# Splitting each mixer pass in two and starting the next pass beside the last delta-rule block, with looser pins on the row steps

## The chip, the cores and the metric

The kernel runs on one core of one Trainium2 chip. The metric is the device time of one execution in microseconds, the median of several runs.

## The reference

One residual block over 1024 tokens of width 1024, in float32, with one layer:

```python
h  = rmsnorm(x)
x += W_out [ gated delta rule, 4 heads x 128 | RG-LRU, 8 groups x 64 ](h)   # the mixer
x += cross_attention(rmsnorm(x), rmsnorm(mem))                              # 4 heads, 256 memory tokens
x += peer(rmsnorm(x))                                                       # 8 heads x 16 experts of 16384
out = rmsnorm(x)
```

In the mixer, q, k and v come from a projection, a causal convolution over 4 positions and SiLU. The delta rule keeps a 128x128 state for each head and goes over the tokens in order. The last part, `peer`, chooses for each token 8 x 16 experts by product keys; every expert is one row of a table `u` and one row of a table `v` (16384 x 1024 each), and adds `gate * gelu(u_e . x) * v_e`.

## The kernel before

**Mixer.** It goes over the tokens in four passes of T = 256 tokens (two blocks of 128). `mixer` (L414) does one pass: transposes of the normalised input (`transposed`, L431), the small projection for gates, twelve projections with convolution (L460; j = 0..3 is q, 4..7 is k, 8..11 is v, each 8 matmuls of 256 columns), a side stream (L472: the z projections and the RG-LRU half), then the delta rule for block b = 0 and block b = 1 (L590), which is a long chain of small matmuls, VectorE (DVE) products and ScalarE (ACT) copies. Then comes the output projection (`out`, L523, 8 weight tiles). While block b = 1 runs, the next input is loaded (L607); after the pass's y is complete it is normalised (L738), and the next pass begins when the output projection is emitted.

**Attention and expert choice.** A second stream, `attended` (L1243), goes over units of tokens (128, 128, 256, 256, 256) once the mixer has finished them: cross-attention, the expert queries, the two-level top-16 (`top16`), and then a choice stream (`choose`, L846).

**Gates.** Tokens 256 to 767 are done densely: over all 16384 experts with a gate matrix that is mostly zero. `gates` (L942) builds that matrix from one-hot products in 32 groups of 16 tokens, and writes each group to DRAM. It begins after the last mixer pass (the mixer's SBUF pool is closed, L1233) and, for each 256 tokens, after their choice is done.

**Dense stage.** `dense` (L1020) goes over 128 slices of 128 experts. Each slice loads a piece of `u` and of `v`, splits both in two halves (DVE `ul`, `vl`), makes 24 matmuls for the hidden values (`dh`), multiplies by gelu and gates (DVE `dg`, `dal`) and makes 24 matmuls for the output (`po`), part of which DVE adds up (`acc`).

**Row steps.** The other 512 tokens (four blocks of 128) are done by gathering rows: for every one of 128 expert slots, an indirect DMA from POOL (`fetch`, L1125) brings 128 rows of `u`, later of `v`, into one of six buffers `rb`, and one DVE instruction of 128x1024 uses it (`step`, L1142): 1024 such steps in all. They are filler: all streams are emitted by a planner that keeps an estimated clock for each engine, and each time the planned TensorE (PE) time has advanced by `pe.pace`, one step is emitted (L115 to L121): every 2800 planned ns in passes 0 to 2, 3500 in pass 3 and in the gates, 2250 in the dense stage. `keep_in_program_order` (L1153, L1164) pins a step behind all DVE work emitted before it; a scheduler that orders each engine's instructions by its own estimate may otherwise move an instruction ahead of work that isn't ready.

**What sets the order.** `together` (L1180) picks among the streams by rank, and among equals by the PE time they had over their share (6 for the mixer and its sides, 1 for attention and choices). A stream that has yielded a wait isn't ready until its engines are, by the planner's clocks.

Of the kernel before, what the change touches and what calls it, by code (L numbers as in the profile page):

```python
# [14 lines left out]
OP = mybir.AluOpType  # L15
AX = mybir.AxisListType

D = 1024
S = 1024
T = 256  # L20
NB = T // 128
NP = S // T
D0 = T
TD = 2 * T
# [13 lines left out]
SHARE = (6.0, 1.0, 6.0, 1.0)  # L38
L_NORM, L_STEP, L_CONV, L_SOFT, L_GATE = 14000.0, 2500.0, 4000.0, 6000.0, 1500.0
PACES = (2800.0, 2800.0, 2800.0, 3500.0)  # L40
PACE_G, PACE_D = 3500.0, 2250.0
FIRST = 0
EARLY = T
UNITS = ((0, 1), (128, 1), (256, 2), (512, 2), (768, 2))
# [5 lines left out]
def block_kernel(ctx: ExitStack, tc: tile.TileContext, a):  # L50
# [21 lines left out]
    class Engine:  # L72

        def __init__(self, engine, fixed, rate):
            self.engine, self.fixed, self.rate = engine, fixed, rate
            self.at = self.total = self.end = 0.0

        def __getattr__(self, op):
            call = getattr(self.engine, op)

            def f(*args, **kw):
                r = call(*args, **kw)  # L82
                aps = [x for x in list(args) + list(kw.values()) if isinstance(x, bass.AP)]
                if op == "dma_start":
                    moved(prod(args[0].shape) * 4)
                else:
                    self.spend(aps)
                return r
            return f

# [314 lines left out]
    def load_x(qkv, t0):  # L405
        for b, t in enumerate(blocks_of(qkv[:, 4:12, :])):
            sp.dma_start(t, a["x"][t0 + b * 128:t0 + (b + 1) * 128, :])

    def norm_x(fp, qkv):
        X = blocks_of(qkv[:, 4:12, :])  # L410
        junk = fp.tile([128, NB, 4, 128], F, name="zs", bufs=1)
        norm(X, NB, X, junk.rearrange("p a b c -> p (a b c)"))

    def mixer(fp, t0, qkv):  # L414
        def conv(ps, ti, w, out, bias=0.0):

            buf = fp.tile([128, T + 3], F, name="cbuf", bufs=CB)
# [7 lines left out]
        def tmp():  # L425
            return fp.tile([128, T], F, name="cy", bufs=CB)

        hT = fp.tile([128, 8, T], F, name="hT", bufs=1)
        if t0 < EARLY:
            hT = Pair(hT, low(0), tmp)  # L430
        yield from transposed(hT, blocks_of(qkv[:, 4:12, :]), NB, wmixc)  # L431
# [25 lines left out]
        dve.tensor_scalar(beta, beta, 1.0, 0.5, op0=OP.add, op1=OP.mult)  # L457


        for j in range(12):  # L460
            ps = yield from proj_T("wA", j, hT, T)
            y = fp.tile([128, T], F, name="cy", bufs=CB)
            conv(ps, j, hcw[:, j, :], y)
            th = fp.tile([128, T], F, name="cth", bufs=1)
            act.activation(th, y, AF.Tanh)
            dve.scalar_tensor_tensor(qkv[:, j, :], th, 1.0, y, op0=OP.add, op1=OP.mult)

        zs = fp.tile([128, NB, 4, 128], F, name="zs", bufs=1)
        yl = fp.tile([128, 4, T], F, name="yl", bufs=1)
        ready = set()  # L470

        def side():  # L472

# [44 lines left out]

        yield Stream(side(), RANK[2], SHARE[2])

        y, x1 = Both(qkv[:, 0:4, :], yl), []

        def out(b0, b1):  # L523

# [65 lines left out]
        for b in range(NB):  # L590
# [14 lines left out]
                act.activation(vb[:, h, :], tv[:, h, :], AF.Copy, scale=beta[:, b, h:h + 1])  # L605
            if b == NB - 1 and t0 + T < S:
                load_x(qkv, t0 + T)  # L607
            yield L_STEP
            pk = b4("tp")
            for h in range(H):  # L610
# [121 lines left out]
            if t0 == 0 and b == 0:  # L732
                yield Stream(out(0, 1), FIRST, SHARE[0])

        while not ready >= {"y", *range(NB)}:
            yield None
        if t0 + T < S:
            norm_x(fp, qkv)  # L738
        yield from out(0 if t0 else 1, NB)
        while t0 not in done:  # L740
            yield None

    def add_cols(X, j, ps):
# [359 lines left out]

    todo, fetched = [], []
    blocks = {}

    def add_block(row, rs, idx, gt):
# [29 lines left out]
    def late_row():  # L1139
        return bool(fetched) and fetched[0][4] > max(dve.at, pe.at) + WAIT  # L1140

    def step():  # L1142
        while todo and len(fetched) < NROW - 1:
            fetch()
        if not fetched:
            return False
        row, ph, k, t, _ = fetched.pop(0)
        B = blocks[row]
        if ph == "u":
            if k == 0:  # L1150
                dve.scalar_tensor_tensor(B["h"], B["h"], B["rs"], B["w"], op0=OP.mult, op1=OP.mult)
                B["hd"] = gat.tile([128, 128], F, name="hdot", bufs=1)
            tc.keep_in_program_order(  # L1153
                dve.scalar_tensor_tensor(t, t, 1.0, B["h"], op0=OP.mult, op1=OP.mult,
                                         accum_out=B["hd"][:, k:k + 1]))
            if k == 120:
                B["x"] = row_of(NROW + 1)
                sp.dma_start(B["x"], x2d[row:row + 128, :])
            if k == 127:
                B["a"] = gat.tile([128, 128], F, name="ga", bufs=1)  # L1160
                act.activation(B["a"], B["hd"], AF.Gelu_apprx_tanh)
                dve.tensor_mul(B["a"], B["a"], B["gt"].rearrange("p h k -> p (h k)"))
        else:
            tc.keep_in_program_order(  # L1164
                dve.scalar_tensor_tensor(B["x"], t, B["a"][:, k:k + 1], B["x"], op0=OP.mult, op1=OP.add))
            if k == 127:
                finish(B["x"], row, t)
        return True
# [58 lines left out]

    def mixed():

        for i in range(NP):  # L1230
            pe.pace = PACES[i]
            yield from mixer(fp, i * T, qkv)
        mix.close()  # L1233
        pe.pace = PACE_G
        yield Stream(gated(), RANK[3], SHARE[3])
# [28 lines left out]
    fps.close()  # L1264
    with tc.tile_pool(name="dn", bufs=1, side="right") as d2, \
            tc.tile_pool(name="dps", bufs=1, space=bass.MemoryType.PSUM) as dps:
        pe.pace, pe.real = PACE_D, False
        dense(dn[0], d2, dps, hT, raws)
    while step():
        pass  # L1270
# [64 lines left out]
```

## Time and profile before

| | us |
|---|---|
| median of 3 runs | 3276.9 |
| range of the runs | 3274.99 to 3279.72 |
| the profiled execution, its own time | 3275.43 |
| its span in the trace | 3273.7 |

| stretch of the span, us | what runs |
|---|---|
| 0 to 341 | pass 0, memory projections, first attention unit |
| 341 to 662 | pass 1, second unit; first row steps |
| 662 to 1009 | pass 2, third unit |
| 1009 to 1341 | pass 3, third and fourth unit |
| 1341 to 1790 | gates, rest of the fourth unit, fifth unit |
| 1790 to 3249 | dense stage |
| 3249 to 3274 | last sums, norms and stores |

PE is busy for 91% of the span, DVE for 84%, ACT for 39%, POOL for 44%. A busy share of a stretch says how full an engine is there, not who waits for whom; for that the views of waits and of the last chain are read beside it.

### The profile page before, as it was taken

What the parts mean: (1) busy time and instruction counts of PE and PEld (TensorE: products, weight loads), DVE (VectorE), ACT (ScalarE), POOL (GpSimd) and SP (SyncE); (2) the same over time, 40 slices, a digit from 0 to 9 for tenths busy, and PEclk for the clock granted to TensorE, in tenths of its full rate; (3) what the DMA queues carried; (4) which work ended last, traced back from release to release, by engine and by line L of the source; (5) the groups of instructions that cost most, each with busy time, mean ns of one, the idle gap of its engine ahead of it and who ended that gap; (6) DMA issues with size and microseconds to landing.
All of it is one profiled execution on the core that took longest, in us unless ns stands there. A gap on an engine that the chain in (4) does not pass through costs nothing.

```text
span 3273.7 us, 46519 instructions
## 1 busy us (share of the span) xinstructions
PE 2987.4 (91%) x16212; PEld 2559.6 (78%) x16212; DVE 2737.6 (84%) x5999; ACT 1277.8 (39%) x2694; POOL 1431.4 (44%) x1046
## 2 busy tenths in 40 slices
PE   6999997699999989898857899999999999999998
PEld 6888887678988878887746677888888878888886
DVE  7634776877787898898999798888999989899998
ACT  6843363236322642376357332222222222222222
POOL 0000233334433344243345375556666655566663
PEclk9999998899999999998968899999999999999999
DMA  5346788688888769888888799999999899999995
GB/s 170 110 143 208 248 281 308 232 285 284 308 292 291 251 223 332 301 281 302 303 289 273 267 329 334 333 340 330 344 333 328 319 334 333 330 341 327 339 331 198
DMA packets 321547, 941.66 MB, mean 288 GB/s; under 512 B 28912, under 2 KB 108832, under 8 KB 319264
## 3 DMA queue, kind: packets, MB, share of 16 engines
q0 software_dynamic: 148048, 538.04, 46.8%
q1 hardware_dynamic: 107216, 367.08, 30.9%
q10 hardware_dynamic: 66048, 33.56, 3.7%
q8 instruction: 128, 2.10, 0.3%
q14 instruction: 107, 0.88, 0.1%
HBM read 894.53 MB, written 44.04 MB: 287 GB/s over the span
## 4 chain that ended last, share of the span: by engine, by line
PE 61%; DVE 20%; DMA 9%; ACT 5%; issue 3%; POOL 1%; SPq 0%; ACTq 0%; DVEq 0%; POOLq 0%
PE dh L106 21%; PE po L106 20%; PE pj L106 15%; DVE rb L82 6%; DMA rb<-in_u,idx 4%; PE gd L106 3%; DVE oh L82 3%; DMA gd<-stage 2%; DMA w<-in_pwq 1%; PE tp L111 1%; PE sc L106 1%; DVE cy L82 1%; ACT ohg L82 1%; DVE i L82 1%; ACT L82 1%
## 5 line engine op out<-in xcount | busy, mean ns | idle before, releaser
L1134 POOL DMA_INDIRECT rb<-in_u,idx x512 | 677.4, 1323 | 1111.9 <-DVE rb L82 497.0
L1134 POOL DMA_INDIRECT rb<-in_v,idx x512 | 745.0, 1455 | 690.3 <-DVE rb L82 478.7
L82 DVE SCALAR_TENSOR_TENSOR rb<-rb 128x1024 f32<-128x1024 f32 x512 | 613.1, 1218 | 90.2 <-DMA rb<-in_u,idx 90.2
L82 DVE SCALAR_TENSOR_TENSOR rb<-rb,ga 128x1024 f32<-128x1024 f32 x512 | 655.0, 1279 | 11.2 <-DMA rb<-in_v,idx 4.9
L106 PE MATMUL pj<-hT,w 128*128 128x256 f32 (+1 forms) x2880 | 590.6, 358 | 16.2 <-DMA w<-in_pwq 11.8
L106 PEld LDWEIGHTS pj<-hT,w 128*128 128x128 f32 x2880 | 491.8, 195 | 73.5 <-DMA w<-in_pwq 13.1
L106 PE MATMUL dh<-hT_h,uh 128*128 128x512 f32 x1024 | 407.1, 398 | 21.4 <-ACT dg L82 20.7
L106 PE MATMUL po<-vh,dah 128*128 128x512 f32 x1024 | 404.8, 395 | 9.7 <-DVE acc L82 8.7
L106 PE MATMUL dh<-hT_l,uh 128*128 128x512 f32 x1024 | 406.2, 397 | 0.0
L106 PE MATMUL dh<-hT_h,ul 128*128 128x512 f32 x1024 | 406.1, 397 | 0.0
L106 PE MATMUL po<-vh,dal 128*128 128x512 f32 x1024 | 405.2, 396 | 0.4 <-DVE dal L82 0.4
L106 PE MATMUL po<-vl,dah 128*128 128x512 f32 x1024 | 405.3, 396 | 0.0
L82 ACT CAST uh<-ur 128x1024 fp32r<-128x1024 f32 x128 | 134.7, 1052 | 561.0 <-PE dh L106 352.8
L106 PE MATMUL gd<-ohg,oh 128*128 128x128 f32 x1024 | 183.7, 332 | 81.4 <-ACT ohg L82 54.5
L106 PEld LDWEIGHTS dh<-hT_h,uh 128*128 128x128 f32 x1024 | 193.2, 189 | 69.3 <-ACT dg L82 21.6
L106 PEld LDWEIGHTS gd<-ohg,oh 128*128 128x128 f32 x1024 | 163.8, 228 | 101.9 <-ACT ohg L82 80.5
L106 PEld LDWEIGHTS po<-vh,dah 128*128 128x128 f32 x1024 | 192.3, 188 | 58.4 <-DVE acc L82 10.0
L106 PEld LDWEIGHTS dh<-hT_h,ul 128*128 128x128 f32 x1024 | 193.0, 189 | 47.0
L106 PEld LDWEIGHTS dh<-hT_l,uh 128*128 128x128 f32 x1024 | 193.2, 189 | 46.4
L106 PEld LDWEIGHTS po<-vl,dah 128*128 128x128 f32 x1024 | 192.3, 188 | 47.2
L106 PEld LDWEIGHTS po<-vh,dal 128*128 128x128 f32 x1024 | 192.3, 188 | 47.1 <-DVE dal L82 0.8
L82 DVE TENSOR_TENSOR ul<-ur,uh 128x1024 fp32r<-128x1024 f32 x128 | 156.0, 1222 | 48.7 <-ACT uh L82 27.6
(339 smaller groups left out, 4757.4 us busy)
## 6 DMA issues: line engine op xcount, KB each, us to landing
ur<-in_ut SPq DMA_DIRECT2D x128, 512.0 KB
vr<-in_v SPq DMA_DIRECT2D x128, 512.0 KB
w<-in_wA SPq DMA_DIRECT2D x80, 512.0 KB
w<-in_pwq SPq DMA_DIRECT2D x80, 512.0 KB
gd<-stage ACTq DMA_DIRECT2D x32, 1024.0 KB
G<-gd SPq DMA_DIRECT2D x16, 2048.0 KB
w<-in_wout SPq DMA_DIRECT2D x40, 512.0 KB
w<-in_wq SPq DMA_DIRECT2D x40, 512.0 KB
```

The source lines that it names most:

```text
L82: r = call(*args, **kw)
L106: self.engine.matmul(out, l, r, **kw)
L111: self.engine.transpose(out, i, ident)
L1134: pool.indirect_dma_start(out=t, out_offset=None, in_=a[ph], in_offset=bass.IndirectOffsetOnAxis(ap=B["idx"][:, k:k + 1], axis=0))
```

## The change

A pass is cut into `heads` (up to and with the side stream) and `delta` (the two blocks, the output projection). A `chain` for pass i runs `heads`, then `delta`; when `delta` comes to its last block it spawns the chain of pass i + 1 as a stream of its own, right behind the load of the next input. The new `heads` waits until the previous pass's side stream is over, sets its pass's pace, normalises the input (with the `hT` buffer as scratch), and makes k and v first (j = 4..11). Before q (j = 0..3, whose buffer holds the previous pass's output) it waits until the previous pass's output projection is emitted.

A row step is no longer pinned behind all DVE work emitted before it. It is pinned behind the previous step and behind the last DVE instruction that the planner ends no later than the row's planned landing plus 1000 ns (`behind`). The constant pace of the dense stage, 2250, becomes 1316000 over the number of steps that are still to come at its start.

```diff
-PACE_G, PACE_D = 3500.0, 2250.0
+PACE_G, DENSE = 3500.0, 1316000.0
...
+    def heads(fp, P, prev, qkv):
...
+        while prev and "y" not in prev.ready:
+            yield None
+        pe.pace = PACES[t0 // T]
         hT = fp.tile([128, 8, T], F, name="hT", bufs=1)
+        if prev:
+            X = blocks_of(qkv[:, 4:12, :])
+            norm(X, NB, X, hT[:, 0:D // T, :].rearrange("p c t -> p (c t)"))
+            yield list(X)
...
-        for j in range(12):
+        for j in (4, 5, 6, 7, 8, 9, 10, 11, 0, 1, 2, 3):
+            while j == 0 and prev and not prev.finished():
+                yield None
...
             if b == NB - 1 and t0 + T < S:
                 load_x(qkv, t0 + T)
+                yield Stream(after(), RANK[1], SHARE[0])
...
-        while not ready >= {"y", *range(NB)}:
-            yield None
-        if t0 + T < S:
-            norm_x(fp, qkv)
         yield from out(0 if t0 else 1, NB)
...
+    def behind(r, land):
+        past = [i for i, t in dve.log[:-1] if t <= land + WAIT][-1:] + steps[-1:]
+        for i in past:
+            tc.add_manual_dep(r.ins, i.name, mybir.DependencyInfo(
+                mybir.DependencyClass.NoSync, mybir.DependencyReason.DATA), reason="rows")
+        steps.append(r.ins)
+        del dve.log[:-200]
...
-            tc.keep_in_program_order(
-                dve.scalar_tensor_tensor(B["x"], t, B["a"][:, k:k + 1], B["x"], op0=OP.mult, op1=OP.add))
+            behind(dve.scalar_tensor_tensor(B["x"], t, B["a"][:, k:k + 1], B["x"],
+                                            op0=OP.mult, op1=OP.add), land)
...
-        for i in range(NP):
-            pe.pace = PACES[i]
-            yield from mixer(fp, i * T, qkv)
+        def chain(i, prev):
+            P = Pass(i * T)
+            yield from heads(fp, P, prev, qkv)
+            yield from delta(fp, P, qkv, lambda: chain(i + 1, P))
+            if i == NP - 1:
+                over.add(0)
...
-        pe.pace, pe.real = PACE_D, False
+        pe.pace, pe.real = DENSE / (2.0 * (S - TD) - stepped[0]), False
```

## Rows read from the trace of the kernel before

**Rows 1.** The page: span, and each engine's busy time, share, instructions

```profile
span 3273.7 us, 46519 instructions
PE 2987.4 (91%) x16212; PEld 2559.6 (78%) x16212; DVE 2737.6 (84%) x5999; ACT 1277.8 (39%) x2694; POOL 1431.4 (44%) x1046
```

**Rows 2.** Windows by stage: stretch, length, busy of each engine (instructions), clock, DMA share

```profile
core 0: us, PE busy (x) PEld busy (x) DVE busy (x) ACT busy (x) POOL busy (x), PEclk, DMA share, GB/s
...
341.00:662.00 321.00, 270.06 (x1779) 247.00 (x1778) 245.47 (x775) 124.92 (x316) 109.71 (x96) 0.90 0.77 271
662.00:1009.00 347.00, 322.34 (x1999) 288.00 (x1997) 272.19 (x731) 133.51 (x330) 138.62 (x121) 0.98 0.83 291
1009.00:1341.00 332.00, 305.80 (x1918) 273.44 (x1916) 281.60 (x901) 135.45 (x331) 119.89 (x101) 0.98 0.78 274
1341.00:1561.00 220.00, 188.14 (x1185) 171.13 (x1184) 196.32 (x614) 143.56 (x392) 76.92 (x66) 0.91 0.87 295
1561.00:1636.00 75.00, 67.80 (x366) 58.72 (x364) 67.14 (x251) 26.64 (x75) 28.42 (x24) 0.95 0.89 309
1636.00:1790.00 154.00, 99.10 (x497) 86.82 (x498) 147.58 (x400) 110.47 (x310) 67.69 (x45) 0.76 0.88 275
1790.00:1835.00 45.00, 24.32 (x91) 18.87 (x92) 26.61 (x42) 14.90 (x18) 10.99 (x10) 0.77 0.78 300
1835.00:3249.00 1414.00, 1403.99 (x6007) 1127.82 (x6006) 1288.96 (x1519) 402.43 (x510) 871.58 (x567) 1.00 0.90 326
3249.00:3274.00 25.00, 11.54 (x50) 8.94 (x48) 19.61 (x75) 6.12 (x12) 0.00 (x0) 0.80 0.26 106
```

**Rows 3.** The last chain between 1780 and 1850 us: start, length, what

```profile
1789.85 21.73 DMA gd<-stage
```

**Rows 4.** Windows of each pass's last block with `out`, and its successor's first projections

```profile
195.00:341.00 146.00, 135.24 (x1112) 129.62 (x1110) 66.30 (x312) 53.66 (x136) 0.00 (x0) 0.99 0.56 183
341.00:387.00 46.00, 43.29 (x247) 35.77 (x246) 32.24 (x114) 20.60 (x53) 8.33 (x8) 1.00 0.69 247
...
546.00:662.00 116.00, 85.61 (x629) 82.03 (x628) 95.55 (x357) 23.30 (x51) 37.94 (x35) 0.84 0.73 259
662.00:706.00 44.00, 38.88 (x198) 30.92 (x196) 29.19 (x87) 14.65 (x37) 13.22 (x14) 0.92 0.75 259
...
868.00:1009.00 141.00, 131.87 (x918) 123.26 (x916) 113.80 (x362) 28.69 (x61) 55.72 (x49) 0.98 0.87 307
1009.00:1056.00 47.00, 46.19 (x249) 38.05 (x248) 33.07 (x79) 14.06 (x40) 12.24 (x13) 1.00 0.81 283
```

**Rows 5.** Groups of instructions: line, engine, what, count; busy us, mean ns; idle before, releasers

```profile
L82 DVE SCALAR_TENSOR_TENSOR rb<-rb,ga 128x1024 f32<-128x1024 f32 x512 | 655.0, 1279 | 11.2 <-DMA rb<-in_v,idx 4.9
L82 DVE SCALAR_TENSOR_TENSOR rb<-rb 128x1024 f32<-128x1024 f32 x512 | 613.1, 1218 | 90.2 <-DMA rb<-in_u,idx 90.2
...
L82 DVE SCALAR_TENSOR_TENSOR cy<-cbuf,hcw,cy 128x256 f32<-128x256 f32 x144 | 69.4, 483 | 3.5 <-ACT cy L82 0.8
...
L82 DVE SCALAR_TENSOR_TENSOR qkv<-cth,cy 128x256 f32<-128x256 f32 x48 | 20.2, 422 | 8.9 <-ACT cth L82 8.2 <-issue 0.6
```

**Rows 6.** The same groups, TensorE's 256-column projections

```profile
L106 PE MATMUL pj<-hT,w 128*128 128x256 f32 (+1 forms) x2880 | 590.6, 358 | 16.2 <-DMA w<-in_pwq 11.8 <-ACT cy L82 1.9 <-DMA w<-in_wq 1.5
```

**Rows 7.** DVE's timeline: the choice that the first gates need ends

```profile
1267.44 0.28 DVE L82 TENSOR_TENSOR e<-oh 128x64 f32<-128x64 bf16 x1
```

**Rows 8.** Window of the rows' tile `rb`, from the dense stage's start (POOL: fetches)

```profile
1790.00:3274.00 1484.00, 0.00 (x0) 0.00 (x0) 730.09 (x842) 3.45 (x6) 882.57 (x577) 0.99 0.89 322
```

**Rows 9.** Waits from 1835 to 3249 us: who for whom, us, times, longest

```profile
DVE rb L82 <- DMA rb<-in_u,idx: 49.1, 27, 5.7
```

**Rows 10.** DVE's timeline at the end: last row steps, their block's and the last output

```profile
3245.52 2.60 DVE L82 SCALAR_TENSOR_TENSOR rb<-rb,ga 128x1024 f32<-128x1024 f32 x2
...
3253.39 1.28 DVE L82 SCALAR_TENSOR_TENSOR rb<-rb,f_y,wfin 128x1024 f32<-128x1024 f32 x1
...
3268.64 1.29 DVE L82 SCALAR_TENSOR_TENSOR acc<-acc,f_y,wfin 128x1024 f32<-128x1024 f32 x1
```

More of the change, by code (lines that the diff above doesn't have):

```diff
@@ L76, in __init__ @@
             self.at = self.total = self.end = 0.0
+            self.log = []
         def __getattr__(self, op):
@@ L87, in f @@
                     self.spend(aps)
+                    self.log.append((r.ins, self.at))
                 return r
@@ L412, in norm_x, with __init__, finished @@
         norm(X, NB, X, junk.rearrange("p a b c -> p (a b c)"))
-    def mixer(fp, t0, qkv):
+    class Pass:
+        def __init__(self, t0):
+            self.t0, self.ready, self.x1 = t0, set(), []
+        def finished(self):
+            return self.t0 in done and (self.t0 > 0 or 128 in done)
+    def heads(fp, P, prev, qkv):
+        t0, ready = P.t0, P.ready
         def conv(ps, ti, w, out, bias=0.0):
@@ L469, in mixer @@
         yl = fp.tile([128, 4, T], F, name="yl", bufs=1)
-        ready = set()
+        P.g, P.beta, P.zs, P.yl = g, beta, zs, yl
         def side():
@@ L519, in mixer, with delta @@
         yield Stream(side(), RANK[2], SHARE[2])
-        y, x1 = Both(qkv[:, 0:4, :], yl), []
+    def delta(fp, P, qkv, after):
+        t0, ready, x1 = P.t0, P.ready, P.x1
+        g, beta, zs, yl = P.g, P.beta, P.zs, P.yl
+        y = Both(qkv[:, 0:4, :], yl)
         def out(b0, b1):
@@ L733, in mixer @@
                 yield Stream(out(0, 1), FIRST, SHARE[0])
-        while not ready >= {"y", *range(NB)}:
-            yield None
-        if t0 + T < S:
-            norm_x(fp, qkv)
         yield from out(0 if t0 else 1, NB)
-        while t0 not in done:
+        while not P.finished():
             yield None
@@ L1101, in dense @@
         finish(acc, row3, xs[0][:, NT - 1, :])
-    todo, fetched = [], []
+    todo, fetched, stepped = [], [], [0]
     blocks = {}
@@ L1140, in late_row @@
         return bool(fetched) and fetched[0][4] > max(dve.at, pe.at) + WAIT
+    def behind(r, land):
[5 more added lines that the diff above has]
+        del dve.log[:-200]
+    steps = []
     def step():
@@ L1146, in step @@
             return False
-        row, ph, k, t, _ = fetched.pop(0)
+        row, ph, k, t, land = fetched.pop(0)
+        stepped[0] += 1
         B = blocks[row]
@@ L1152, in step @@
                 B["hd"] = gat.tile([128, 128], F, name="hdot", bufs=1)
-            tc.keep_in_program_order(
-                dve.scalar_tensor_tensor(t, t, 1.0, B["h"], op0=OP.mult, op1=OP.mult,
-                                         accum_out=B["hd"][:, k:k + 1]))
+            behind(dve.scalar_tensor_tensor(t, t, 1.0, B["h"], op0=OP.mult, op1=OP.mult,
+                                            accum_out=B["hd"][:, k:k + 1]), land)
             if k == 120:
@@ L1163, in step @@
         else:
-            tc.keep_in_program_order(
-                dve.scalar_tensor_tensor(B["x"], t, B["a"][:, k:k + 1], B["x"], op0=OP.mult, op1=OP.add))
+            behind(dve.scalar_tensor_tensor(B["x"], t, B["a"][:, k:k + 1], B["x"],
+                                            op0=OP.mult, op1=OP.add), land)
             if k == 127:
@@ L1228, in mixed @@
     def mixed():
-        for i in range(NP):
-            pe.pace = PACES[i]
-            yield from mixer(fp, i * T, qkv)
+        def chain(i, prev):
[4 more added lines that the diff above has]
+                over.add(0)
+        over = set()
+        yield Stream(chain(0, None), RANK[1], SHARE[0])
+        while not over:
+            yield None
         mix.close()
```

## The prediction

> **What bounds the kernel now.** I read the busy shares first, only to see that two engines are nearly full: PE 91% and DVE 84% of the span [rows 1]. An average over stages says nothing of a change in one of them, so the windows by stage come next [rows 2]. The reader is to see three regimes there. In the dense stage, 1835 to 3249, PE is busy for 1404.0 of 1414 us at full granted clock: PE sets it, and only 10 us are lost; DVE is at 1289.0, with 125 us to spare. In the passes, 341 to 1341, PE is busy for 898 of 1000 us (270.1 + 322.3 + 305.8) and DVE for 799, so neither is full, and the delta rule's chain of small steps leaves holes: 51, 25 and 26 us of PE in the three stretches. The first of them also has the granted clock at 0.90, which at the two levels 2.4 and 1.2 GHz means a fifth of the time at the lower one. From 1341 to 1790, where the gates are made, DVE is the fuller engine: 411 of 449 us against PE's 355. The gates are last there, and the dense stage can't run freely until their last write has landed: the chain of work that ended last has a write of 21.7 us at 1789.9 [rows 3], and 1790 to 1835 has only 24.3 us of PE work in 45.
>
> So a gain has to come from the holes before 1790. The dense stage's 1414 us, the 45 us ahead of it and the last 25 us are not shortened by anything that the change moves.
>
> **Part 1: heads beside the last block.** What is moved are the normalisation, the transposes, the gate projection and eight of twelve projections of passes 1 to 3. They stood alone with other streams in the head stretches of 46, 44 and 47 us, and come to stand beside the last block and its output projection, 146, 116 and 141 us [rows 4]. Nothing is removed. The eight projections are 64 matmuls at 590.6 us / 2880 = 0.205 us, 13.1 us of PE for each pass [rows 6], and eight times three convolution products at 0.483 and one at 0.422 us, 15.0 us of DVE [rows 5]. Their eight weight loads go through SP's queue and now compete with the attention's weights and the rows; DMA is at 0.73 to 0.87 in these blocks and at 0.69 to 0.81 in the head stretches [rows 4], so together they fit, but not with much over.
>
> If chain length alone counted, 46 + 44 + 47 = 137 us would go. It doesn't: attention and choices fill these stretches too, and their work remains. So I ask how short each pair of stretches can be when the fuller engine in it is at 97%, which PE all but reaches in 1009 to 1056 (46.2 of 47). Pass 0 to 1: 192 us hold 178.5 us of PE work, 184 are needed, gain 8. Pass 1 to 2: 160 us hold 124.5 of PE and 124.7 of DVE (of which rows are part), 129 are needed, gain 31. Pass 2 to 3: 188 us hold 178.1, 184 are needed, gain 4. That makes 43 us; the floor is nothing, if the chain's own waits stay. Of the 31 in the middle I take two thirds, 21, because the block's chain gets longer when its DVE and ACT steps queue behind the convolutions; the other two are small already. **Gain 33 us, bounds 0 and 43.** By the granted clock there is a little more in it: 546 to 662 ran at 0.84 [rows 4], so at full clock its 85.6 us of PE would be 71.9, 14 us that only count if DVE isn't what limits. I keep 14 for the range.
>
> Whether this reaches the end: by conservation it does. When the mixer ends sooner, attention has got no further, and the gates share DVE with it for longer; but the work that is done at any time is ahead by what the holes gave. The first gates also need the choice of tokens 256 to 511; its last DVE product is at 1267.7 [rows 7], 73 us before 1341, so the gates can move up by that much before this wait takes the place of the mixer's.
>
> **Part 2: how many steps are left for the dense stage.** Of the 1024 fetches 577 are issued after 1790 [rows 8], 447 before. Steps are emitted by planned PE time. A front shorter by 33 us has 33 x 121 / 347 = 12 fewer at the rate of pass 2, and the slower pace of pass 3 starts when its heads do, up to 141 us earlier: (121 / 347 - 101 / 332) x 141 = 6 fewer [rows 2, 4]. So 18 more lie in the dense stage, 18 x 1.29 = 23 us of DVE (a u row is 1.218 + 0.081 for reading the sum, a v row 1.279 [rows 5]). Cover: the 125 us in which DVE idles there. If that cover were gone, they would cost their 23 us. I take 3, since 10 us of PE were lost there with more room. The new pace only spreads them to the end: at 577 to 600 steps it is 2281 to 2193 planned ns against 2250, about as now.
>
> **Part 3: the end.** The last two steps now run at 3245.5 and their block's norm at 3253.4, while the last output is normed at 3268.6 [rows 10]. The constant 1316000 puts the last step nearer the end: 577 x 2250 is 1298250, so the steps end later by up to 18 planned us of a stage that takes 1459, though not behind it. In 3249 to 3274 DVE is busy for 19.6 of 25 us [rows 2]; two rows and a norm there are some 4 us more, of which part is hidden. **Cost 3 us, bounds 0 and 6.**
>
> **Part 4: looser pins.** The same instructions run; only DVE's fixed order changes, and with it when POOL may refill a buffer. What DVE's order is after that no row of before shows. Bounds: the best is that rows fill DVE's idle time in the gates, 38 us of 449; the worst is that rows come up before they have landed. Behind a row that waits stands all later DVE work (`ul`, `dg`, `dal`, `acc`, and the delta rule's products), and PE, ACT and POOL's next fetch wait for those. The nearest rows are the two kinds of steps themselves: u rows made DVE wait for 90.2 us, v rows for 4.9 [rows 5], at the same distance of fetch to use. As the planned landing goes into the pins, I take 0, and keep -15 (less than half the idle time) and +60 (worked out below).
>
> The Trainium skill (Perfetto Trace Analysis, section Tensor Engine Instruction) says that ACT, DVE and GpSimd are strict FIFO. That speaks against this part, as an unlanded row can't be overtaken; the waits of DVE for u rows are of that kind, and no run here shows a DVE instruction that passes another.
>
> **Sum.** 3275.4 (the profiled execution; the median of the runs is 1.5 above it) - 33 + 3 + 3 + 0 = **3248 us**, 0.8% less.
>
> **The rivals.** (a) *The holes don't fill.* The last block's chain gets longer by what the heads take, or the gates wait for the choice, which now gets less PE time (share 1 against two mixer streams of 6). Then the front gains 0 to 8 us and parts 2 and 3 cost as much: 3273 to 3281, 3277 in the middle. For it speaks that two of three pairs of stretches are at 93 and 95% of PE already. The same time comes out where the overlap is planned but the scheduler orders it as before.
>
> (b) *More than that.* All three passes pack better, the clock of the first stays up, and rows fill DVE's gaps in the gates: half of the 102 us of PE holes, 14 us of clock and 10 of the gates: 3275 - 75 = 3200. Against it: DMA at 0.77 to 0.83 in the passes already, and DVE at 91% in the gates [rows 2].
>
> (c) *Slower: rows that stand unlanded in DVE's queue in the dense stage.* There u rows cost 49.1 us in 27 waits [rows 9], and PE hardly felt it, since DVE had 125 us left. If v rows come to wait as u rows do, that is 49 us more, and with 23 us for the moved steps 72 of the 125 are gone; if each kind waits twice as often as u rows now, 49 x 3 = 147 more, and 147 + 23 - 125 = 45 us show in PE, plus some 40 in the front, where 41 us of such waits (90.2 - 49.1) double. With the gain of 33 taken off that is 3275 + 45 + 40 - 33 + 6 = 3333; at the point from which it decides, 125 us of new waits and moved steps together, it is still a tie with part 1's gain. A milder form, in which u and v waits double in the front alone and break the chain there, gives about 3290. For it: six buffers give no more distance of fetch to use than before. Against: the pin that is left holds a row back by its planned landing.
>
> **How the numbers follow.** Forecast (3225 to 3265): 0.50. Rival (b), 3180 to 3225: 0.15. Rival (a), 3265 to 3285: 0.18. Rival (c), 3285 to 3335: 0.17. A measurement of this kernel tells 0.2% (6.6 us) from no change. Faster are the forecast, (b) and a small part of (a): 0.67; the same, 3270 to 3283, is most of (a): 0.14; slower is (c) and the rest of (a): 0.19. The range leaves out the lower half of (b) and the upper half of (c): 3200 to 3300. The forecast's own range is 3225 to 3265.
>
> **What would show it.** Right: the first gate products (`gd` from `ohg`) some 30 us sooner, weight loads of pass i + 1 between the last block's steps of pass i, PE holes of 341 to the mixer's end well under 102 us, the dense stage beginning near 1757 and as long as before within 10 us, 590 to 600 fetches behind its start, DVE's waits for rows at 60 to 130 us in all. Wrong: the dense stage longer by over 20 us or PE there waiting for `acc`, `dal` or `ul` (rival c); the dense stage's start unmoved though the mixer ends earlier (rival a, or the choice as the new wait); the front shorter but its steps fewer by over 100, which DVE couldn't take in the dense stage.

## The result

The changed kernel takes 3233.6 us (median; 3226.2 to 3245.1) where the kernel before takes 3278.3 beside it: a ratio of 0.9865, 95% interval 0.9846 to 0.9885. The profiled execution of after takes 3238.5 us, so the 36.9 us to before's 3275.4 are a fair picture of the change. The page of after first, to be read against [rows 1]:

```profile
span 3236.7 us, 46492 instructions
PE 2982.7 (92%) x16212; PEld 2554.5 (79%) x16212; DVE 2723.6 (84%) x5999; ACT 1281.2 (40%) x2694; POOL 1454.7 (45%) x1046
```

Each engine runs as many instructions as before, and the busy times agree within 0.6%, POOL's within 2%. What changed is when they run. The windows by stage (columns as in [rows 2]: stretch, length, then busy time of PE, PEld, DVE, ACT and POOL, granted clock, DMA share, GB/s); stages are cut as there, at the issue of each pass's last output-projection weights and at the first `dh` of the dense stage:

```profile
334.00:651.00 317.00, 290.14 (x2065) 266.69 (x2066) 242.64 (x914) 130.61 (x344) 78.64 (x73) 0.97 0.78 273
651.00:966.00 315.00, 302.32 (x1943) 272.55 (x1942) 256.69 (x715) 136.78 (x328) 125.56 (x109) 1.00 0.84 294
966.00:1283.00 317.00, 293.49 (x1865) 266.41 (x1863) 265.38 (x854) 122.41 (x292) 116.50 (x97) 0.97 0.78 273
1283.00:1731.00 448.00, 348.71 (x2016) 314.87 (x2016) 409.56 (x1301) 281.57 (x771) 168.59 (x135) 0.86 0.88 291
1731.00:1776.00 45.00, 37.57 (x134) 29.19 (x135) 30.51 (x43) 18.84 (x22) 14.46 (x10) 0.84 0.81 292
1776.00:3212.00 1436.00, 1406.24 (x5965) 1125.95 (x5964) 1325.25 (x1557) 399.12 (x505) 943.33 (x606) 0.99 0.92 336
3212.00:3237.00 25.00, 11.24 (x49) 8.69 (x47) 19.48 (x76) 6.86 (x12) 0.00 (x0) 0.80 0.26 106
```

Pass 0 ends 7 us sooner (334 for 341), the three passes shrink from 1000 to 949 us (4, 32 and 15 us in turn), the gates stage stays (449, now 448), the stretch from 1776 to 3212 takes 1436 where its counterpart took 1414, and the last 25 us are as before. From the start of the dense stage to its last `po` it is 1491 us against 1470. So the front gave 58 us (dense stage from 1731.5 in place of 1789.9) and the dense stage took 21 back: 37.

In [rows 5] the row steps waited 90.2 us for `u` rows and 4.9 for `v` rows; the groups of after (busy, mean ns, idle before and what ended most of it), with the `po` matmuls that wait for DVE's `acc`, and as the last line the same matmuls in before:

```profile
L83 DVE SCALAR_TENSOR_TENSOR rb<-rb,ga 128x1024 f32<-128x1024 f32 x512 | 655.8, 1281 | 29.5 <-DMA rb<-in_v,idx 23.9
L83 DVE SCALAR_TENSOR_TENSOR rb<-rb 128x1024 f32<-128x1024 f32 x512 | 611.2, 1218 | 31.4 <-DMA rb<-in_u,idx 31.3
L108 PE MATMUL po<-vh,dah 128*128 128x512 f32 x1024 | 408.5, 399 | 27.7 <-DVE acc L83 27.7
L106 PE MATMUL po<-vh,dah 128*128 128x512 f32 x1024 | 404.8, 395 | 9.7 <-DVE acc L82 8.7 <-ACT dah L82 1.0
```

Waits for rows fell from 95 to 55 us in all. That is the opposite of what I had feared of the looser pins, and the first sign that the gain isn't where I had put it.

### The profile page after: what moved, and what is told of

Its sections match the earlier page's. It is cut to its first block, busy times and chain, and to the rows that moved or that the text cites. A ratio compares the mean times of both kernels' runs of the same rounds, so it can differ in the third digit from the quotient of the medians.

```text
span 3236.7 us, 46492 instructions
## 1 busy us (share of the span) xinstructions
PE 2982.7 (92%) x16212; PEld 2554.5 (79%) x16212; DVE 2723.6 (84%) x5999; ACT 1281.2 (40%) x2694; POOL 1454.7 (45%) x1046
## 4 chain that ended last, share of the span: by engine, by line
PE 49%; DVE 25%; DMA 12%; issue 7%; ACT 5%; POOL 2%; SPq 0%; another core or an unknown queue 0%; DVEq 0%; POOLq 0%; ACTq 0%
PE dh L108 15%; PE po L108 14%; PE pj L108 14%; DVE rb L83 8%; PE gd L108 4%; DMA rb<-in_v,idx 4%; DVE oh L83 3%; DMA gd<-stage 2%; POOL rb L1157 2%; DMA rb<-in_u,idx 2%; PE tp L113 1%; DVE i L83 1%; DMA w<-in_pwq 1%; PE sc L108 1%; DVE dg L83 1%
## 5 line engine op out<-in xcount | busy, mean ns | idle before, releaser
L1157 POOL DMA_INDIRECT rb<-in_u,idx x512 | 701.2, 1369 | 1104.2 <-DVE lxf L83 419.7
L83 DVE SCALAR_TENSOR_TENSOR rb<-rb,ga 128x1024 f32<-128x1024 f32 x512 | 655.8, 1281 | 29.5 <-DMA rb<-in_v,idx 23.9
L108 PEld LDWEIGHTS pj<-hT,w 128*128 128x128 f32 x2880 | 491.0, 195 | 70.8 <-DMA w<-in_pwq 14.5
L108 PE MATMUL po<-vh,dah 128*128 128x512 f32 x1024 | 408.5, 399 | 27.7 <-DVE acc L83 27.7
L108 PEld LDWEIGHTS dh<-hT_h,ul 128*128 128x128 f32 x1024 | 194.4, 190 | 50.6 <-DVE ul L83 2.9
L83 ACT CAST dah<-dg 128x512 fp32r<-128x512 f32 x128 | 79.6, 622 | 305.1 <-DVE dg L83 302.4
```

Source lines behind the costliest of these rows:

```text
L108: self.engine.matmul(out, l, r, **kw)
L1157: pool.indirect_dma_start(out=t, out_offset=None, in_=a[ph], in_offset=bass.IndirectOffsetOnAxis(ap=B["idx"][:, k:k + 1], axis=0))
```

## The experiments

The change has three separable parts: the **overlap** of the next heads with the last block, the **pins**, and, as a side effect of the overlap, **fewer row steps ahead of the dense stage** (404 in place of 444, counted as DVE steps before the first `dh`). The paces set that last number, so all three can be switched apart. In the table "passes" is from the end of pass 0 to the end of pass 3, "PE idle" what PE wasn't busy there, "dense" from the first `dh` to the last `po`, "u, v" DVE's waits for rows in the whole run, "acc" the wait of `po` for `acc`; the ratio is to the kernel before on the same chip, with its 95% interval. All but the median and the ratio come from the one profiled execution of each kernel, and those of e1, e2 and e7 were 10 to 15 us slower than their medians. How far single profiles scatter shows in e5: up to the first slices of the dense stage each of its engines has the instructions of after in the same order, and yet it begins that stage at 1721.4 us, after at 1731.5. So a difference of under some 10 us between stages of two profiles shows nothing by itself.

| kernel | order, pins | median | ratio | front steps | passes (PE idle) | dense | u, v | acc |
|---|---|---|---|---|---|---|---|---|
| before | sequential, old | 3276.6 to 3282.3 | 1 | 444 | 1000 (102) | 1470 | 90, 5 | 9 |
| e3_fewer_rows | sequential, old | 3267.8 | 0.9963 [0.9945, 0.998] | 404 | 989 (88) | 1498 | 116, 16 | 28 |
| e2_pins_only | sequential, new | 3258.8 | 0.993 [0.9909, 0.9952] | 446 | 988 (99) | 1477 | 30, 14 | 16 |
| e6_pins_fewer | sequential, new | 3251.6 | 0.9915 [0.9886, 0.9944] | 408 | 966 (73) | 1505 | 31, 19 | 30 |
| e7_heads_more | overlap, old | 3303.2 | 1.0067 [1.0044, 1.009] | 436 | 1054 (128) | 1473 | 140, 12 | 9 |
| e1_pins_back | overlap, old | 3281.6 | 1.0009 [0.999, 1.0027] | 400 | 994 (88) | 1499 | 100, 14 | 24 |
| e4_more_rows | overlap, new | 3254.6 | 0.992 [0.9903, 0.9937] | 443 | 1004 (90) | 1480 | 29, 14 | 23 |
| after | overlap, new | 3233.6 | 0.9865 [0.9846, 0.9885] | 404 | 949 (63) | 1491 | 31, 24 | 28 |
| e8_slower_paces | overlap, new | 3228.0 | 0.9851 [0.9827, 0.9876] | 375 | 919 (55) | 1501 | 38, 18 | 36 |
| e10_latest | overlap, old pin and chain | 3238.9 | 0.9885 [0.985, 0.992] | 400 | 958 (71) | 1473 | 23, 6 | 9 |
| e9_no_landing | overlap, chain alone | 3350.1 | 1.0228 [1.0196, 1.026] | 512 | 1037 (121) | 1541 | 72, 46 | 71 |
| e5_pace_back | overlap, new, old dense pace | 3260.8 | 0.9945 [0.9922, 0.9968] | 404 | 946 | 1466 | 15, 19 | 10 |

**The overlap without the pins.** e1 is after with the old pin:

```diff
-        past = [i for i, t in dve.log[:-1] if t <= land + WAIT][-1:] + steps[-1:]
-        for i in past:
-            tc.add_manual_dep(r.ins, i.name, ...)
-        steps.append(r.ins)
-        del dve.log[:-200]
+        tc.keep_in_program_order(r)
```

> The changed kernel with the old pins: every row step again behind all DVE work emitted before it; heads beside the last block and the dense pace stay, and the planned order and number of steps are the same. Two questions. Front: after reached its dense stage at 1731.5 us, before at 1789.9. If the heads' overlap (or the fewer steps in the front) made that, it stays at 1725 to 1740; if the looser pins made it, it goes back towards 1760 to 1790. Dense stage: after took 1480 us (1731.5 to 3211.6), before 1459. If the 40 more steps there cost the 21 us, it stays near 1480; if rows that come up too early cost them, it goes back to 1459 to 1465. Overlap and steps: 3230 to 3240. Overlap and pins: 3212 to 3220. Pins made the front: 3255 to 3290.

It takes what before takes. The whole gain is gone with the pins, though the overlap and the 44 steps moved to the dense stage are all there. Its dense stage is longer than after's (1499 us), where I had put it at as long or shorter. e7 gives the front its steps back, by faster paces:

```diff
-PACES = (2800.0, 2800.0, 2800.0, 3500.0)
+PACES = (2500.0, 2500.0, 2500.0, 3100.0)
```

> The heads beside the last block with the old pins and faster paces (2500, 2500, 2500, 3100): some 436 to 444 steps in the front, as before. It differs from before by the overlap alone, at equal steps and pins. If the overlap by itself gains what part 1 said (33 us), it is at 3240 to 3255; if the old pins undo it, as with 400 steps (3282), it is at 3275 to 3300 and TensorE's waits for DVE in the passes are at 40 us or over.

At nearly equal steps (436 and 444) and with old pins the overlap alone is a loss of 0.67%, some 21 us, and the time is just above the 3275 to 3300 that I had given. In the passes PE waits 66 us for DVE, 51 in before (sums over the view of PE's waits).

**The pins without the overlap.** e2 is before with `behind` and its log; e6 the same with the paces of e3.

```diff
-            tc.keep_in_program_order(
-                dve.scalar_tensor_tensor(t, t, 1.0, B["h"], ...))
+            behind(dve.scalar_tensor_tensor(t, t, 1.0, B["h"], ...), land)
```

> The kernel before with the looser pins alone; passes, paces and the number of steps in front (444) and dense stage (580) as before. If pins do little: dense stage from 1780 to 1792 on, 1455 to 1465 long, total 3265 to 3280. If pins shorten the front: dense stage from 1760 to 1775, total 3245 to 3262. If pins cost in the dense stage: it takes 1475 to 1485, total 3285 to 3300.

> The kernel before, passes one after the other, with the looser pins and slower paces (3000, 3000, 3000, 4000): 404 steps in the front, as many as after. Pins alone gave 3259, fewer steps alone 3268, all three parts 3234. If pins and fewer steps make the whole gain, this is at 3230 to 3242 with the dense stage from 1735 to 1745 us on; if the overlap of the heads is needed too, 3246 to 3256 and from 1748 to 1762 on.

The pins are a gain by themselves, 0.70% at 446 steps and 0.48% at 404 to 408 (e6 against e3), but half or a third of what they bring with the overlap: 1.47% (e4 against e7) and 1.44% (after against e1). e6's time is the one I had given for the case that the overlap is needed too (3246 to 3256), but its dense stage begins at 1730.0, not at 1748 to 1762; what that says of the overlap stands in part 1 below.

**The number of front steps.** e3 is before, and e4 after, with other paces:

```diff
-PACES = (2800.0, 2800.0, 2800.0, 3500.0)
-PACE_G, PACE_D = 3500.0, 2250.0
+PACES = (3000.0, 3000.0, 3000.0, 4000.0)
+PACE_G, PACE_D = 3500.0, 2122.0
```

> The kernel before with slower paces in the passes (3000, 3000, 3000, 4000), so that 40 steps fewer are emitted in the front (404, about as many as after has) and 620 in the dense stage (pace 2122); passes one after the other and old pins. If the fewer steps made after's front shorter (40 x 1.29 = 52 us of DVE), the dense stage starts at 1740 to 1755; if the overlap did, at 1780 to 1795. If 40 more steps cost the dense stage 21 us, it takes 1475 to 1485, else 1455 to 1465. Overlap and steps: 3285 to 3300. Steps alone: 3245 to 3260.

> The changed kernel with faster paces in the passes (2500, 2500, 2500, 3100): some 436 steps in the front and 588 in the dense stage, nearly the numbers of before. If the overlap made the front shorter and DVE has room there: dense stage from 1735 to 1745 on, 1460 long, total 3215 to 3230, a gain on after. If fewer steps made the front shorter, the dense stage starts at 1765 to 1785 and the total is 3245 to 3270.

(e4 has the paces of e7.) Forty steps fewer in the front are worth 0.37% (e3) and 0.55% (after against e4); in the other two pairs 0.15% (e6 against e2, within their intervals) and 0.58% (e1 against e7). In e3's profile the dense stage starts 35 us sooner and is 28 us longer, more than the 21 that I had allowed for, so that e3's time lies between the two ranges I had given. e8 goes on in this direction, after with paces of 3000 and 4000:

> The changed kernel with slower steps in the front: one per 3000 planned ns in passes 0 to 2 and per 4000 in pass 3 (2800 and 3500 in the changed kernel), so about 369 steps ahead of the dense stage in place of 404 and about 655 in it. Theory A (a step in the front costs about 0.9 us because DVE's order matters there, and one in the dense stage about 0.5 us as long as DVE has room): the front is some 30 us shorter, the dense stage 18 us longer, 3220 to 3228 in all. Theory B (the dense stage has no more room: DVE was busy for 1325 of 1436 us there, and 35 more steps are 45 us of DVE): the dense stage takes back 30 us or more, 3230 to 3250; then DVE's busy share in it is over 0.95 and PE waits for acc or for the halves of u and v.

It has the lowest median of all, 3228.0, but its interval and after's lie across each other, so it isn't shown to be better. The front gave 27 more, the dense stage took 10 (1501), and DVE in 1750 to 3196 is busy for 0.937 of the time, just under the 0.95 of theory B. So it comes out nearly as theory A had it:

```profile
1750.00:3196.00 1446.00, 1407.35 (x5963) 1124.91 (x5962) 1355.17 (x1584) 399.72 (x506) 972.61 (x634) 0.99 0.93 344
```

**Does the sequence leave holes at all?** Both kernels with the row steps left out, but for five of each block and phase, which keep the blocks' ends (the unused sums are set to zero):

```diff
-        todo.extend((row, ph, k) for ph in "uv" for k in range(128))
+        todo.extend((row, ph, k) for ph, k in (("u", 0), ("u", 120), ("u", 127), ("v", 0), ("v", 127)))
```

> The kernel before with five row steps for each of its four blocks instead of 256 (the other steps and their fetches are left out, the hidden values set to 0): the passes' packing without the filler. No end of it was measured. The dense stage should be PE's 1434 us; the front loses 444 x 1.29 = 573 us of DVE work: some 1500 to 1650 us, total 2970 to 3110. It stands beside the same cut of the changed kernel, and their difference is what tells.

> The changed kernel with the same cut to five row steps for each block. With no row steps, pins and paces have nothing to act on, so the difference to the cut kernel of before is the overlap alone. If the overlap fills holes of the delta rule's chain (part 1), it is 25 to 45 us shorter; if the holes stay and the gain came from how the steps are placed, 0 to 10 us. If it is over 50, the steps take some of it back.

3060.3 and 3071.8 us: without rows the overlap is 11.5 us slower, and I had given no range for a loss. The windows of the passes in before, then passes, gates and dense stage of n_before, then of n_after:

```profile
341.00:1341.00 1000.00, 898.20 (x5690) 808.44 (x5688) 799.27 (x2406) 393.88 (x977) 368.23 (x316) 0.96 0.80 279
```

```profile
340.00:1220.00 880.00, 845.38 (x5604) 767.36 (x5603) 458.91 (x1866) 397.12 (x979) 10.09 (x10) 0.99 0.40 133
1220.00:1602.00 382.00, 341.87 (x2150) 312.38 (x2150) 280.59 (x1148) 276.48 (x774) 1.41 (x2) 0.94 0.57 168
1602.00:3044.00 1442.00, 1437.54 (x6144) 1154.35 (x6142) 661.36 (x761) 421.34 (x534) 12.84 (x10) 1.00 0.36 123
```

```profile
336.00:1209.00 873.00, 830.76 (x5640) 760.33 (x5639) 460.73 (x1923) 388.50 (x956) 9.81 (x10) 0.98 0.42 139
1209.00:1605.00 396.00, 357.18 (x2249) 326.52 (x2248) 292.91 (x1227) 278.08 (x778) 1.41 (x2) 0.95 0.57 169
1605.00:3056.00 1451.00, 1440.33 (x6144) 1156.98 (x6144) 660.51 (x760) 421.59 (x535) 13.90 (x10) 1.00 0.36 122
```

This is the reading that matters most. The very same sequence, without rows, leaves PE idle for 880 - 845 = 35 us of the passes, not 102. Two thirds of the holes that I had taken for room between the passes went with the row steps and their fetches. Who ended PE's waits there says more, summed over the view of PE's waits: 50.6 us for DVE, 27.6 for ACT and 22.1 for DMA in before; 16.3, 14.5 and 3.2 in n_before. So half of what went (34 of 67 us) were waits for DVE, and 19 us were waits for DMA, mostly for weights, with a DMA share of 0.80 in before and 0.40 here. The cut takes out the steps on DVE and the rows' transfers together; which of them made how much isn't shown beyond that. The longest wait for DVE and the longest for DMA, in before and in n_before:

```profile
PE tp L111 <- DVE go L82: 14.1, 4, 11.6
PE pj L106 <- DMA w<-in_pwq: 8.7, 3, 5.0
```

```profile
PE tp L111 <- DVE go L82: 6.9, 3, 6.0
PE pj L106 <- DMA w<-in_pwq: 3.2, 2, 2.5
```

And the overlap doesn't fill the rest: 42 us are idle in n_after. The passes end 7 us shorter with 15 us less of PE work in them, the gates stage is 14 us longer with 15 us more of it, so the heads' work only changed its place. The dense stage is 9 us longer.

**Which part of the new pin.** It consists of a landing (behind a DVE instruction planned to end by then) and a chain (behind the previous step). Both are order-only edges: they fix the order of two instructions in DVE's program and make nothing wait. e9 keeps the chain alone, e10 the chain and, in place of the landing, the DVE instruction emitted just before the step, which is where the old pin stood:

```diff
-        past = [i for i, t in dve.log[:-1] if t <= land + WAIT][-1:] + steps[-1:]
+        past = steps[-1:]
```

```diff
-        past = [i for i, t in dve.log[:-1] if t <= land + WAIT][-1:] + steps[-1:]
+        past = [i for i, t in dve.log[:-1]][-1:] + steps[-1:]
```

> The changed kernel with each row step pinned behind the previous step alone; the pin behind the last DVE instruction that is planned to end by the row's landing is left out. Theory A (what gained was that a step no longer stands behind all DVE work emitted before it, and the landing hardly binds): the time is the changed kernel's within 0.3%, 3225 to 3243, and DVE waits for rows as little as there, 55 us in all. Theory B (the landing in the pin is what keeps unlanded rows out of DVE's queue): DVE's waits for rows grow to 130 us or more, and the time to 3250 or more, as the forecast's slower rival had it.

> The changed kernel with the row step pinned behind the previous step and behind the DVE instruction emitted just before it, whatever the row's landing: the old pin plus the chain of steps. The pin of the kernel before is the same without the chain. Theory A (the gain lies in how early a step may stand: by the planner's clocks the landing lies some 11 us before the step's emission in the front, and the landing pin is typically 17 DVE instructions back): this kernel is as slow as the overlap with the old pins, 3265 to 3290, with DVE waiting for u rows for 80 us or more. Theory B (the chain from step to step is what brought it): within 0.3% of the changed kernel, 3225 to 3243.

e10 decides it: theory A, mine, falls. The old pin with the chain is at 0.9885, all but 0.2% of after's gain, and the two intervals lie across each other. **The chain is what brought it**: e1 and e10 differ in the chain alone, and it is worth 1.24%, some 41 us. In the passes PE waits 37.9 us for DVE in e1 and 26.1 in e10, for ACT 20.1 and 12.3, for DMA 28.5 and 29.0: what the chain took away there is mostly waiting for DVE, and none of it for DMA. e10 begins its dense stage 28 us sooner than e1 and needs 26 less for it (e1's profile is 10 us above its median). The groups of e1 and of e10:

```profile
L83 DVE SCALAR_TENSOR_TENSOR rb<-rb 128x1024 f32<-128x1024 f32 x512 | 611.6, 1218 | 100.7 <-DMA rb<-in_u,idx 100.3
L83 DVE SCALAR_TENSOR_TENSOR rb<-rb,ga 128x1024 f32<-128x1024 f32 x512 | 655.3, 1280 | 20.4 <-DMA rb<-in_v,idx 13.9
```

```profile
L83 DVE SCALAR_TENSOR_TENSOR rb<-rb,ga 128x1024 f32<-128x1024 f32 x512 | 655.3, 1280 | 12.7 <-DMA rb<-in_v,idx 6.2
L83 DVE SCALAR_TENSOR_TENSOR rb<-rb 128x1024 f32<-128x1024 f32 x512 | 606.0, 1218 | 24.0 <-DMA rb<-in_u,idx 22.9
L108 PE MATMUL po<-vh,dah 128*128 128x512 f32 x1024 | 406.9, 397 | 9.0 <-DVE acc L83 8.6
```

Why a chain? The old pin ties a step to the DVE instruction emitted just before it, and to nothing else; the section on the kernel before says "behind all DVE work emitted before it", and that is more than it does. The next step isn't tied to this one. Every `v` step adds to the same `x`, so the data keep those in order. A `u` step writes its own column of the sums, so nothing did. The expert slots in the order in which DVE's program has them, first block's `u` steps, as before was built:

```
0 1 2 3 4 5 6 7 8 9 10 11 12 13 14 17 15 16 18 19 20 22 21 23 ... 41 44 42 43 45
```

POOL's fetches stand in an order of their own (..., 20, 23, 21, 22, 24, ...), since the scheduler places a fetch when a buffer comes free. Slot 17 in DVE's timeline of before, and POOL's fetches beside it (start, length, what, in brackets the idle time before and what ended it):

```profile
414.22 1.27 DVE L82 SCALAR_TENSOR_TENSOR rb<-rb 128x1024 f32<-128x1024 f32 x1
415.42 1.21 DVE L82 SCALAR_TENSOR_TENSOR rb<-rb 128x1024 f32<-128x1024 f32 x1
...
416.97 0.16 DVE L82 TENSOR_SCALAR g_i<-g_ss 128x8 int32<-128x8 int32 x1
420.69 1.23 DVE L82 SCALAR_TENSOR_TENSOR rb<-rb 128x1024 f32<-128x1024 f32 x1 [3.56 <-DMA rb<-in_u,idx]
...
421.85 0.17 DVE L82 TENSOR_SCALAR g_y<-g_i 128x8 int32<-128x8 int32 x1
...
423.92 0.68 DVE L82 TENSOR_TENSOR g<-tp,g_y 128x512 f32<-128x512 f32 x1
...
425.46 1.22 DVE L82 SCALAR_TENSOR_TENSOR rb<-rb 128x1024 f32<-128x1024 f32 x1
426.60 1.22 DVE L82 SCALAR_TENSOR_TENSOR rb<-rb 128x1024 f32<-128x1024 f32 x1
```

```profile
409.46 1.01 POOL L1134 DMA_INDIRECT rb<-in_u,idx  x1 [2.09 <-DVE hist L82]
411.15 0.94 POOL L1134 DMA_INDIRECT rb<-in_u,idx  x1 [0.68 <-DVE rb L82]
412.69 0.94 POOL L1134 DMA_INDIRECT rb<-in_u,idx  x1 [0.60 <-DVE rb L82]
...
422.20 0.94 POOL L1134 DMA_INDIRECT rb<-in_u,idx  x1 [3.51 <-DVE cbuf L82]
426.95 1.68 POOL L1134 DMA_INDIRECT rb<-in_u,idx  x1 [3.81 <-DVE rb L82]
```

Rows 15, 16 and 17 are fetched at 409.5, 411.2 and 412.7. DVE stands still from 417.1 to 420.7 for row 17, 8.0 us behind its fetch. Behind it stand the normalisation of the delta rule's block (`g_y`, then `g`) and rows 15 and 16, which are used only at 425.5 and 426.6, 16.0 and 15.5 us behind theirs; the fetch at 422.2 is slot 23's, into row 17's buffer, while theirs stay taken, and the fetch of slot 21, at 427.0, after 3.8 us of idle POOL, is released by row 15's step. So a row out of order is paid twice: by DVE at once, and by the fetches that need the buffers of those it passed.

This can be counted, by laying the two programs' orders beside the trace. In before 156 of the 512 `u` steps stand ahead of a row that was fetched earlier, on average 10.7 us behind their own fetch, and the other 356 are 16.7 us behind theirs. **Of the 44 waits for `u` rows over 0.3 us, 40 are of those 156, and they hold 82.4 of 89.2 us.** In e1 it is 162 steps with 95.7 of 99.2 us, in e7 171 with 120.5 of 139.6. With a chain next to nothing is out of order (after 6 steps, e10 7), and what is left, 25 and 18 us, are rows that come in order.

e9 shows what the other half of the pin is for. With the chain alone the scheduler put 512 steps ahead of the dense stage and the rest close together behind it. Passes, gates, the dense stage up to its last row, and the rest of it:

```profile
335.00:1372.00 1037.00, 916.08 (x5871) 819.97 (x5869) 905.30 (x2737) 394.00 (x967) 501.67 (x419) 0.96 0.89 327
1372.00:1791.00 419.00, 342.26 (x2017) 308.95 (x2018) 373.53 (x1151) 276.13 (x768) 134.43 (x95) 0.89 0.79 264
1791.00:2964.00 1173.00, 1097.70 (x4569) 871.69 (x4569) 1082.30 (x1335) 320.51 (x404) 743.61 (x512) 0.97 0.93 343
2964.00:3331.00 367.00, 367.00 (x1575) 295.14 (x1574) 162.77 (x184) 102.47 (x132) 0.00 (x0) 1.00 0.32 107
```

With 512 rows crowded into 1173 us PE loses 75 us there; in the 367 us without rows it loses none. Its time is theory B's (3350, and 118 us of row waits where I had written 130), but the cause isn't only an unlanded row: a step needs some lower bound on its place, or it comes too early. Either bound does: the landing, or the place where it was emitted.

**The pace of the dense stage.** e5 is after with the constant:

```diff
-        pe.pace, pe.real = DENSE / (2.0 * (S - TD) - stepped[0]), False
+        pe.pace, pe.real = 2250.0, False
```

> The changed kernel with the constant pace of the dense stage back, one step per 2250 planned ns, in place of 1316000 over the steps left (620 steps, 2123). Theory A (the new pace is needed because 40 more steps are left): about 33 steps are left over when the dense stage's matmuls end and follow alone at 1.3 us each, 40 us or more behind it: 3265 to 3285. Theory B (the pace makes no difference, since the scheduler packs steps into DVE's free time whatever the planner's pace): the changed kernel's time within 0.3%, 3225 to 3243.

```profile
1721.00:3187.00 1466.00, 1446.48 (x6142) 1159.64 (x6143) 1317.43 (x1569) 420.07 (x531) 900.22 (x583) 0.99 0.90 326
3187.00:3260.00 73.00, 0.75 (x4) 0.26 (x2) 62.34 (x106) 4.60 (x8) 39.66 (x32) 0.52 0.78 278
```

As theory A had it: 32 fetches and 62 us of DVE work are left when PE has ended, and the time is 27 us over after's, somewhat below the 3265 that I had given as its lower end. The new pace belongs to the moved steps: without it the last of them follow behind the last matmul.

## Why the prediction was right in its number and wrong in its reasons

The number, 3248 in 3200 to 3300, holds 3233.6, and faster was the likeliest case. Two of its terms are wrong, in opposite directions, so that the number holds is luck. Along the way before, e7, e1, after, the 1.35% are: overlap +0.67, forty fewer front steps -0.58, pins -1.44. Along another way (before, e2, e6, after) they are pins -0.70, steps -0.15, overlap -0.50. The parts act on each other, so none has a price of its own.

**What bounds the kernel.** The regimes were right: the dense stage is PE's, with DVE's room to spare, and the gain came before 1790. The step that failed is the sentence on the passes: that "the delta rule's chain of small steps leaves holes: 51, 25 and 26 us of PE" [rows 2]. n_before has the same chain and 35 us of holes in the place of 102. The view of DVE's waits in these 1000 us would have given a hint, though no more: its longest line is rows, ahead of every single wait for PE or ACT. Beside these waits the row steps keep DVE busy for 385 us of the 1000, and what PE needs of DVE queues behind them.

```profile
DVE rb L82 <- DMA rb<-in_u,idx: 32.3, 17, 3.6
DVE X L82 <- PE pj L106: 28.3, 16, 7.1
DVE s L82 <- PE sc L106: 23.7, 14, 5.8
```

**Part 1, gain 33.** Its mechanism fell. Alone it costs 21 us (e7), and 11.5 with no rows in the way. The bound of nothing as its floor was wrong too: I had let the chain's waits stay, but not let what the heads displace come back in the gates, where n_after has 357 us of PE work in 396 us and n_before 342 in 382. The clock came as I had kept it for the range: the first stretch has 0.97 in place of 0.90. With the chained pins the overlap is worth 0.10% (e4 against e2) to 0.50% (after against e6); of these the second alone is larger than 0.2%. Even there the profiles show no gain in the front: after's passes end 24 us sooner than e6's (1283 for 1307), but its gates stage takes 448 us for 423, and the two begin the dense stage at 1731.5 and 1730.0. By the profiles, which scatter by some 10 us, the difference lies behind that (dense 1491 for 1505), where the overlap moves nothing; why is open. A reading was off too: the DMA share of the three last blocks is 0.56 to 0.87 [rows 4], not 0.73 to 0.87.

**Part 2, 18 more steps for 3 us.** It was 40 (577 fetches behind the dense stage's start became 615), in part because the first row step came at 434 us in place of 367: at one step per 2.8 us of pace these 67 us are some 24 steps, by estimate, and the rest goes with the shorter front. That the front is then shorter stands nowhere in the sum, and it is the larger effect: 35 us of front for 28 of dense stage in e3. The cover was right in kind: e10 has 624 steps in the dense stage, 44 more than before, and takes 1473 us, 3 more. With the old pins it fails: at 620 and 624 steps e3 and e1 take 1498 and 1499. The 21 us that after loses there come with its landing pin: `v` rows wait for 23.9 us in place of 4.9, and `po` for `acc` 27.7 in place of 8.7.

```profile
DVE rb L83 <- DMA rb<-in_u,idx: 22.2, 9, 6.0
DVE rb L83 <- DMA rb<-in_v,idx: 20.6, 12, 4.8
...
PE po L108 <- DVE acc L83: 27.7, 11, 5.0
```

(These are the waits of after in 1776 to 3212, us in all, times, longest; `u` had 49.1 in 27 in [rows 9].) That is **rival (c)** in small: the mechanism exists, at some 18 us (1491 less e10's 1473, one profile each), and the gain of the chain hid it. In the whole it went the other way.

**Part 3, cost 3.** Nothing: the last 25 us are the same, and the last row steps end at 3212.1, before the last output's norm at 3231.3, as in [rows 10]:

```profile
3208.21 3.92 DVE L83 SCALAR_TENSOR_TENSOR rb<-rb,ga 128x1024 f32<-128x1024 f32 x3
...
3231.33 1.29 DVE L83 SCALAR_TENSOR_TENSOR acc<-acc,f_y,wfin 128x1024 f32<-128x1024 f32 x1
```

That the pace stays "about as now" fell with the 40 steps: it is 1316000 / 620 = 2123, and with the old one 73 us would follow the last matmul.

**Part 4, 0 with bounds of -15 and +60.** This is the term that carried the result, and it lies outside its bounds: -47 us beside the overlap (3281.6 to 3233.6), -23 without (0.70% of 3278). The step that failed is one sentence: that u rows waited 90.2 us and v rows 4.9 "at the same distance of fetch to use". On average the distance was the same (14.9 us for `u` rows, 14.7 for `v`), but not from step to step, and the asymmetry had a cause in the program: `x` orders the one kind and nothing the other, and the `u` steps that had passed others came 6 us closer behind their fetch than the rest. The words "behind the previous step" stand in my description of the change, and I priced only the other half, the landing, which is worth 0.2%, within the uncertainty. The rule of the Trainium skill (Perfetto Trace Analysis, section Tensor Engine Instruction) that DVE is strict FIFO agrees with the 3.56 us at 420.7; I had weighed it against this change, and it speaks for it, since it is the old order of that queue that was bad.

**The signs I had named.** The first gate products came 50 us sooner, not 30:

```profile
1309.43 1.95 PE L108 MATMUL gd<-ohg,oh 128*128 128x128 f32 x16
```

```profile
1359.01 1.95 PE L106 MATMUL gd<-ohg,oh 128*128 128x128 f32 x16
```

(The first line is after's, the second before's.) The dense stage began at 1731.5, not 1757, and was 21 us longer, not under 10; DVE's waits for rows, 55 us, are below the 60 to 130.

**What stays open.** Why the new pins bring 47 us beside the overlap and 16 to 23 in the sequence, where chain and landing weren't taken apart. PE's holes in the passes go from 128 to 90 by the pins with the overlap (e7, e4) and from 102 to 99 without (before, e2), though the `u` waits fall by much in both. The waits of steps out of order don't tell the two apart: e3, sequential, has 107.3 us of them at 404 front steps, e1 95.7 at 400. Not tried: the landing pin in the front and e10's pin in the dense stage, which by the two profiles would take 15 us from e10's front.

## What to carry to other kernels

When two kinds of the same filler instruction wait very differently, ask which dependence orders the one and not the other: a scheduler may reorder instructions that share a ring of buffers but no data, and each one ahead of its fetch stops its engine and then the fetches. A chain of order-only edges from one step to the next is cheap and was worth more than the whole overlap; it needs a lower bound on each step's place besides. And before holes of an engine are counted as room for another order of stages, take the filler out once: here two thirds of the holes went with it and its transfers.
